# Tying the low parts of causal-attention weights behind the head's scaling on VectorE

## The chip, the cores and the metric

The kernel runs on one core of a Trainium2 chip. The metric is the device time in microseconds, the median of the runs; the kernel before took 1104.67 us (three runs, 1104.64 to 1106.62).

## What is computed

Two layers over 512 tokens of width 1024, in fp32. Layer A mixes tokens by spatial gating, layer B by causal "forgetting" attention with 12 heads of 64; both add attention to a memory of 256 rows (4 heads), a projection back, and a gated feed-forward part of width 2816. The change lies in layer B, of which this is the core:

```python
s_in = rmsnorm(h, ln_shared)
kvf = s_in @ w_shared_kv                 # keys, values, forget gates
k_s = kvf[..., :MAIN_WIDTH].reshape(B, S, FOX_HEADS, HEAD_DIM)
v_s = kvf[..., MAIN_WIDTH:2 * MAIN_WIDTH].reshape(B, S, FOX_HEADS, HEAD_DIM)
log_f_s = jax.nn.log_sigmoid(kvf[..., 2 * MAIN_WIDTH:] + b_forget)
...
logits = jnp.einsum('bthd,bshd->bhts', qi, k).astype(jnp.float32) * scale
logits = logits + ci[..., :, None] - cT[..., None, :]     # c: cumulated log_f
logits = jnp.where(mask, logits, -jnp.inf)
p = jax.nn.softmax(logits, axis=-1).astype(v.dtype)
return jnp.einsum('bhts,bshd->bthd', p, v)
```

## The kernel before

Activations lie transposed, features on the partitions, in tiles of 128 x 512. Each fp32 product is made of three fast ones (mm3, L189 to L193): both factors are split into a high part (a cast to fp32r by ScalarE) and a low part (the rest, a subtraction on VectorE), and high x high, high x low and low x high are added up in PSUM. The split is the helper `split` (L238): `A.copy(hi, src)` and then `tensor_sub(lo, src, hi)`, on VectorE unless told otherwise. In the profile the parts of a weight are called whi and wlo, and the freshly loaded weight raw.

Weights come by `prepared` (L147): a DMA from SP's queue into one of four raw buffers of 128 x 1024, then `weight_parts` (L155), which splits it in steps of 512 columns into whi and wlo tiles; there are eight buffers of each. Weights of another layout, those of the output and of the down projection, go through `moving_pair` (L164), which calls `split` itself. A raw buffer is free for the next load when both of its halves have been cast and subtracted.

In layer B the attention runs over heads in `attend` (L539): four heads on the memory, then the 12 causal heads (FoxHead, L498). For each head the steps stand in a written order:

```python
steps = ("T0", "S3", "F0", "T1", "S2", "N3", "F1", "V0", "S1", "N2", "T2", "F2", "S0", "N1", "V1", "N0",
         "F3", "V2", "F4")
```

S3 to S0 are the logits of the four blocks of 128 queries, the longest row first: two products on TensorE (L513, L514), mask and row maximum in one VectorE instruction (L443), the exponential with its sum on ScalarE (L445). N2 and N0 (`norm`, L448) invert the sums of two blocks (L453) and scale their probabilities (L458): N2 those of blocks 3 and 2, of which block 3 is scaled on ScalarE (L456, by_scalar), N0 those of blocks 1 and 0, both on VectorE. T and V belong to the head before: T0 to T2 transpose its scaled probabilities on TensorE (L465) and split them into pT, V0 to V2 multiply them with the values (L533); behind V2 the output is joined (L423, L424). F0 to F4 are places for other work. They take the copies of queries and keys for heads to come (`pair_split`, `head_parts`, L1342 to L1360, eight small DMAs a head on SP), and pieces of the fill queue: the products of the key blocks (L1240) and value blocks (L1266), cut in 48 pieces, from which heads take 5, 5, 5, 5 (the memory heads), 4, 4, 4, 4, 3, 3, 3, 3 (the first eight causal ones), and then of the output projection. `queue` (L214) lists the load of a block, with its splits, three pieces ahead of the block's first. The fill queue is value block 0, keys 0 and 1, value block 1, keys 2 and 3, value block 2, keys 4 and 5.

The order in which the program lists instructions isn't the order in which an engine gets them. When the kernel is built, a scheduler simulates the engines and gives each of them, among the listed instructions whose inputs and buffers are there, the earliest listed one. So instructions that are listed late are put ahead of earlier ones that still wait for something. `tc.issue_after(ins)` (in the helper `behind`, L247) is the tool against that: whatever is listed in its block for the same engine as `ins` is put in that engine's queue behind `ins`. It adds no semaphore and concerns no other engine. An engine works its queue off in the order given.

Of the kernel before, what the change touches and what calls it, by code (L numbers as in the profile page):

```python
# [40 lines left out]
def hybrid(ctx: ExitStack, tc: tile.TileContext, i: dict, out: bass.AP):  # L41
# [8 lines left out]
    pp = ctx.enter_context(tc.tile_pool(name="psum", bufs=3, space=PSUM))  # L50

    n_of = {}
    last_load, last_exp, last_parts = [None], [None], [None, None]

    def name(s):
        n_of[s] = n_of.get(s, 0) + 1
# [20 lines left out]
    V, A, PE, G = nc.vector, nc.scalar, nc.tensor, nc.gpsimd  # L77
# [53 lines left out]
    def pair_of_parts(n=512, aside=False):  # L131
        if aside:
            return act("whi"), act("wlo")
        return (wp.tile([P, max(n, 512)], F32R, tag="hi", name=name("whi"), bufs=8)[:, :n],
                wp.tile([P, max(n, 512)], F32R, tag="lo", name=name("wlo"), bufs=8)[:, :n])

    def cut(pair, w):

        return [(pair[0][:, d : d + w], pair[1][:, d : d + w]) for d in range(0, pair[0].shape[1], w)]
# [7 lines left out]
    def prepared(src, shape, aside=False):  # L147

        raw = wp.tile([P, 1024], F32, tag="raw", name=name("raw"), bufs=4)
        n = shape[0] * shape[1]  # L150
        dst = raw[:, :n].rearrange("p (a b) -> p a b", a=src.shape[1]) if len(src.shape) == 3 else raw[:, :n]
        last_load[0] = nc.sync.dma_start(dst, src)
        return weight_parts(raw, shape, aside)

    def weight_parts(raw, shape, aside=False):  # L155
        n = shape[0] * shape[1]
        parts = []
        for d in range(0, n, 512):
            pair = pair_of_parts(min(512, n - d), aside)
            split(raw[:, d : min(d + 512, n)], *pair)  # L160
            parts += cut(pair, shape[1])
        return parts

    def moving_pair(src, aside=False):  # L164

        raw = wp.tile([P, 1024], F32, tag="raw", name=name("raw"), bufs=4)
        last_load[0] = nc.sync.dma_start(raw.rearrange("p (m c) -> p m c", m=4), src)
        four = raw.rearrange("p (m k c) -> p m k c", m=4, k=2)
        parts = []
        for x in range(2):  # L170
            hi, lo = (t.rearrange("p (m c) -> p m c", m=4) for t in pair_of_parts(aside=aside))
            split(four[:, :, x, :], hi, lo)
            parts.append((hi, lo))
        return parts
# [60 lines left out]
            for dst, src in src_dst:  # L235
                nc.sync.dma_start(dst, src)

    def split(src, hi, lo, eng=None):  # L238
        last_parts[:] = A.copy(hi, src), (eng or V).tensor_sub(lo, src, hi)  # L239

    def scaled_parts(src, g, hi, lo):

# [3 lines left out]
    @contextmanager  # L246
    def behind(some):  # L247

        with ExitStack() as s:
            for ins in some:  # L250
                s.enter_context(tc.issue_after(ins.ins))
            yield
# [124 lines left out]
    def mem_project(layer, xs, wk):  # L377
        keys = []
        wv = [prepared(i["w_mem_v"][layer, kh], (4, 256)) for kh in range(2)]
        for m in range(2):  # L380
            [o] = group([wk[m]], xs, (0, NMEM), ["mm"])
            kf = temp("memk", (P, NMEM))
            V.tensor_mul(kf, o, rmem)
            for j in range(2):
                own, other = rows(j)
                both = act("memk", shape=(P, 2, NMEM))
                A.copy(both[own, 0, :], kf[own, :])
                V.tensor_sub(both[own, 1, :], kf[own, :], both[own, 0, :])
                if layer:
                    G.dma_start(both[other, :, :].bitcast(F32), both[own, :, :].bitcast(F32))  # L390
                else:
                    A.copy(both[other, 0, :], kf[own, :])
                    V.tensor_sub(both[other, 1, :], kf[own, :], both[own, 0, :])
                keys.append(both)
        vals = []
        for mt in range(2):
            o = ps("mm", (P, 256), s="memv")
            for k in range(KT):
                w = wv[k // 4][k % 4]
                mm3(o, (xs[k][0][:, mt * P : (mt + 1) * P], xs[k][1][:, mt * P : (mt + 1) * P]),  # L400
                    w, k == 0, k == KT - 1)
            vf = temp("memv", (P, 256))
            A.activation(vf, o, AF.Copy, scale=r4m[:, mt : mt + 1])
            vals.append(act("memv", shape=(P, MH, 2, 64)))
            split(vf.rearrange("p (a b) -> p a b", a=MH), vals[mt][:, :, 0, :], vals[mt][:, :, 1, :])
        return keys, vals
# [20 lines left out]

    class Softmax:

        by_scalar = ()  # L430

        def __init__(self):
            self.nmx, self.sm = small("nmx"), small("sm")
# [14 lines left out]
        def norm(self, tb):  # L448

            if tb % 2:  # L450
                return
            with ExitStack() if tb else tc.high_priority():
                V.reciprocal(self.sm[:, tb : tb + 2], self.sm[:, tb : tb + 2])  # L453
                for x in (tb + 1, tb):
                    if x in self.by_scalar:
                        A.activation(self.p[x], self.p[x], AF.Copy, scale=self.sm[:, x : x + 1])  # L456
                    else:
                        V.tensor_scalar_mul(self.p[x], self.p[x], self.sm[:, x : x + 1])  # L458

        def turn(self, n, pieces):  # L460

# [36 lines left out]
    class FoxHead(Softmax):  # L498

        TURNS = ((0,), (1, 3), (2,))  # L500
        by_scalar = (3,)

        def __init__(self, pr, j, vals, dst):
            super().__init__()
# [996 lines left out]
```

## Time and profile before

| | |
|---|---|
| median of three runs | 1104.67 us (1104.64 to 1106.62) |
| profiled execution | 1104.15 us, span 1102.4 us |
| TensorE's granted clock | 0.999 |
| causal heads | about 612 to 720 us of the span |
| scalings of the causal heads on VectorE (L458) | 36, 278 to 421 ns each |
| wlo<-raw on VectorE (L239), whole kernel | 460, median 685 ns |
| 512 KB weight loads on SP in 560 to 725 us | 17 |

PE is TensorE's multiplying and PEld its weight load, which runs beside it; DVE is VectorE, ACT ScalarE, SPq the DMA queue of SyncE. A row of the timeline has start and duration in us, the engine, the line in the kernel, the operation, output<-inputs by the program's names with shapes, and a count where equal ones in a row are merged; in brackets stands how long the engine was idle before it and what ended that. A row of the waits says who waited for what, the total in us, how often, and the longest. The lines themselves stand in the prediction, where they are used.

### The profile page before, as it was taken

The page shows a single profiled execution, that of the slowest core. Times are in us where ns is not written, and L with a number is a line of the kernel's source. Part 1 is how long each engine was busy: PE and PEld are TensorE (multiplying, and loading weights), DVE is VectorE, ACT ScalarE, POOL GpSimd, SP SyncE. Part 2 cuts the span into 40 slices and gives each one's busy share as a digit, 9 for nine tenths or more (in the row PEclk, how much of TensorE's full clock was granted, in tenths as well). Part 3 has the DMA queues.
Part 4 walks back from the last instruction along what each step waited for, and adds up shares of the span by engine and source line. Part 5 has one row for each costly group of instructions (what it writes and reads, how often), then busy time and mean ns, then how long its engine had stood idle before and what let it go on. Part 6 is the DMA issues. An engine that isn't in the chain of part 4 may idle for free.

```text
span 1102.4 us, 19497 instructions
## 1 busy us (share of the span) xinstructions
PE 1094.9 (99%) x7362; PEld 1001.0 (91%) x7363; DVE 887.8 (81%) x1750; ACT 679.7 (62%) x1428; POOL 23.9 (2%) x40
## 2 busy tenths in 40 slices
PE   9999999999999999999999999999999999999998
PEld 8998889999899899998988998889999899899996
DVE  7879759997698488797968789868997698588776
ACT  7776578664365254477747788868665266255454
POOL 0000000000000000001000000000000000000000
PEclk9999999999999999999999999999999999999999
DMA  7521331334135133245222654531235134233232
GB/s 271 160 78 58 115 115 39 116 115 138 54 115 148 53 106 115 77 153 175 73 80 61 154 130 125 148 115 40 78 97 153 58 114 132 62 114 117 77 97 77
DMA packets 64021, 118.65 MB, mean 108 GB/s; under 512 B 5236, under 2 KB 40072, under 8 KB 63928
## 3 DMA queue, kind: packets, MB, share of 16 engines
q1 hardware_dynamic: 63032, 116.57, 34.7%
q8 instruction: 58, 0.95, 0.4%
q0 software_dynamic: 192, 0.52, 0.2%
q10 hardware_dynamic: 704, 0.32, 0.1%
q14 instruction: 35, 0.29, 0.1%
HBM read 105.23 MB, written 2.10 MB: 97 GB/s over the span
## 4 chain that ended last, share of the span: by engine, by line
PE 95%; DVE 2%; ACT 2%; DMA 0%; issue 0%; SPq 0%; DVEq 0%; ACTq 0%
PE y L191 10%; PE y L192 10%; PE y L193 10%; PE a L191 5%; PE a L193 5%; PE a L192 5%; PE ps L191 4%; PE ps L193 4%; PE ps L192 4%; PE e L191 3%; PE e L193 3%; PE e L192 3%; PE x L193 3%; PE x L191 3%; PE x L192 3%; PE v L191 2%
## 5 line engine op out<-in xcount | busy, mean ns | idle before, releaser
L239 ACT CAST whi<-raw 128x512 fp32r<-128x512 f32 x460 | 277.6, 620 | 260.3 <-PE y L193 118.5
L239 DVE TENSOR_TENSOR wlo<-raw,whi 128x512 fp32r<-128x512 f32 x460 | 306.3, 686 | 116.8 <-ACT whi L239 114.7
L191 PE MATMUL y<-whi,fhi 128*128 128x512 f32 (+1 forms) x356 | 139.6, 393 | 0.0
L193 PE MATMUL y<-whi,flo 128*128 128x512 f32 (+1 forms) x356 | 139.4, 391 | 0.0
L192 PE MATMUL y<-wlo,fhi 128*128 128x512 f32 (+1 forms) x356 | 139.2, 391 | 0.0
L193 PE MATMUL x<-xshi,wlo 128*128 128x256 f32 x320 | 89.8, 281 | 0.0
L191 PE MATMUL x<-xshi,whi 128*128 128x256 f32 x320 | 89.7, 280 | 0.0
L191 PE MATMUL a<-xshi,whi 128*128 128x256 f32 x320 | 89.7, 281 | 0.0
L192 PE MATMUL a<-xslo,whi 128*128 128x256 f32 x320 | 89.7, 280 | 0.0
L192 PE MATMUL x<-xslo,whi 128*128 128x256 f32 x320 | 89.7, 280 | 0.0
L193 PE MATMUL a<-xshi,wlo 128*128 128x256 f32 x320 | 89.6, 281 | 0.0
L193 PEld LDWEIGHTS y<-whi,flo 128*128 128x128 f32 x356 | 66.9, 188 | 15.6 <-DVE flo L239 0.2
L192 PEld LDWEIGHTS y<-wlo,fhi 128*128 128x128 f32 x356 | 66.9, 188 | 14.9 <-DVE wlo L239 0.2
L191 PEld LDWEIGHTS y<-whi,fhi 128*128 128x128 f32 x356 | 66.9, 188 | 14.7 <-ACT fhi L239 0.2
L191 PE MATMUL ps<-xshi,whi 128*128 128x256 f32 (+1 forms) x224 | 68.4, 305 | 0.0
L192 PE MATMUL ps<-xslo,whi 128*128 128x256 f32 (+1 forms) x224 | 66.7, 298 | 0.0
L193 PE MATMUL ps<-xshi,wlo 128*128 128x256 f32 (+1 forms) x224 | 66.3, 298 | 0.0
L191 PEld LDWEIGHTS a<-xshi,whi 128*128 128x128 f32 x320 | 60.3, 188 | 0.3
L192 PEld LDWEIGHTS a<-xslo,whi 128*128 128x128 f32 x320 | 60.2, 188 | 0.4
L191 PEld LDWEIGHTS x<-xshi,whi 128*128 128x128 f32 x320 | 60.2, 188 | 0.0
L193 PEld LDWEIGHTS x<-xshi,wlo 128*128 128x128 f32 x320 | 60.2, 188 | 0.0
L193 PEld LDWEIGHTS a<-xshi,wlo 128*128 128x128 f32 x320 | 60.2, 188 | 0.0
(303 smaller groups left out, 3075.1 us busy)
## 6 DMA issues: line engine op xcount, KB each, us to landing
raw<-in_w_gate SPq DMA_DIRECT2D x44, 512.0 KB, 3.6
raw<-in_w_up SPq DMA_DIRECT2D x44, 512.0 KB, 3.6
raw<-in_w_down SPq DMA_DIRECT2D x44, 512.0 KB, 4.0
raw<-in_w_out SPq DMA_DIRECT2D x16, 512.0 KB, 4.0
raw<-in_w_b_q SPq DMA_DIRECT2D x8, 512.0 KB, 4.3
raw<-in_w_a_v SPq DMA_DIRECT2D x6, 512.0 KB, 8.1
raw<-in_w_a_u SPq DMA_DIRECT2D x6, 512.0 KB
raw<-in_w_v SPq DMA_DIRECT2D x6, 512.0 KB, 3.5
```

Of the source, the lines that this page charges most:

```text
L191: PE.matmul(o, w[0], x[0], start=start, stop=False, skip_group_check=more)
L192: PE.matmul(o, w[0], x[1], start=False, stop=False, skip_group_check=more)
L193: return PE.matmul(o, w[1], x[0], start=False, stop=stop, skip_group_check=more)
L239: last_parts[:] = A.copy(hi, src), (eng or V).tensor_sub(lo, src, hi)
```

## The change

`split` gets a flag, pinned, which `weight_parts` sets. With it the VectorE subtraction is listed behind the last scaling of a causal head; the high part on ScalarE is listed as before. The list last_scaling is shared with FoxHead and overwritten with each VectorE scaling that `norm` lists; the memory heads have a list of their own that nobody reads. Until the first causal head lists a scaling, it is empty.

```diff
-    last_load, last_exp, last_parts = [None], [None], [None, None]
+    last_load, last_exp, last_parts, last_scaling = [None], [None], [None, None], []
...
         for d in range(0, n, 512):
             pair = pair_of_parts(min(512, n - d), aside)
-            split(raw[:, d : min(d + 512, n)], *pair)
+            split(raw[:, d : min(d + 512, n)], *pair, pinned=True)
             parts += cut(pair, shape[1])
...
-    def split(src, hi, lo, eng=None):
-        last_parts[:] = A.copy(hi, src), (eng or V).tensor_sub(lo, src, hi)
+    def split(src, hi, lo, eng=None, pinned=False):
+        first = A.copy(hi, src)
+        with behind(last_scaling if pinned else ()):
+            last_parts[:] = first, (eng or V).tensor_sub(lo, src, hi)
...
     class Softmax:
-        by_scalar = ()
+        by_scalar, scaled = (), []
...
-                        V.tensor_scalar_mul(self.p[x], self.p[x], self.sm[:, x : x + 1])
+                        self.scaled[:] = [V.tensor_scalar_mul(self.p[x], self.p[x], self.sm[:, x : x + 1])]
...
     class FoxHead(Softmax):
         TURNS = ((0,), (1, 3), (2,))
-        by_scalar = (3,)
+        by_scalar, scaled = (3,), last_scaling
```

## Prediction

> **What bounds the kernel now.** I read the page first, then the stretch in which the change acts by windows and by the waits, then the order of VectorE's queue there in the timeline.
>
> ```profile
> span 1102.4 us, 19497 instructions
> PE 1094.9 (99%) x7362; PEld 1001.0 (91%) x7363; DVE 887.8 (81%) x1750; ACT 679.7 (62%) x1428; POOL 23.9 (2%) x40
> ```
>
> TensorE (PE) is busy for 1094.9 of 1102.4 us. The profiled execution took 1104.15 us, 1.75 us of it outside the span; the median of the runs is 1104.67 us, 0.52 us above it. I work out differences within the span and add them to the median.
>
> The causal heads run from 612 to 720 us. In a row of the windows view the columns are the stretch, its length, then the busy time of PE, PEld (weight load), DVE (VectorE) and ACT (ScalarE). Below it stand the waits in the same stretch in which VectorE can have a part, the total first, then how often and the longest.
>
> ```profile
> 611.00:712.00 101.00, 100.36 (x623) 87.96 (x622) 88.96 (x254) 86.00 (x213) 0.00 (x0) 1.00 0.53 137
> PEld o L533 <- DVE pT L239: 1.5, 5, 0.6
> PEld tr L465 <- PE k L193: 0.6, 1, 0.6
> PE tr L465 <- DVE p L458: 0.2, 1, 0.2
> PE o L533 <- DVE pT L239: 0.2, 1, 0.2
> ```
>
> VectorE has 88.96 us of work in 101 us, so some 12 us are free there, and TensorE is idle for only 0.64 us. TensorE or its weight load waits for VectorE by name for 1.5 + 0.2 + 0.2 = 1.9 us (the 0.6 us row is the same instant as the 0.2 us wait of tr). So 1.9 us is the most that any better order on VectorE can win in this stage, and 1104.67 - 1.9 = 1102.8 us the end of the range below. A wait of VectorE itself, however long, costs nothing until one of these rows grows.
>
> What a measurement of this kernel can tell from no change is about 0.2%, or 2.2 us: faster means below 1102.5 us and slower above 1106.9 us. The largest gain that the waits allow is already inside "the same".
>
> **Which instructions the change moves.** Only weight_parts gets pinned=True, and the list that it ties to is empty until the first causal head has scaled. From then on it holds the last scaling that VectorE was given. Five loads of the fill queue are listed in that time: key blocks 2 and 3 at piece 21 (head 0) and 25 (head 1), both value weights of block 2 at piece 29 (head 2), key blocks 4 and 5 at piece 37 (head 4) and 41 (head 5). I count the causal heads from 0. With attend's steps the first three come in F2, behind N2, whose VectorE scaling is that of block 2; the last two come in F3 and F4, behind N0. Each load of 1024 columns gives two low parts (wlo), so twelve are tied. The output weights go through moving_pair and aren't; the gate and up weights after the last head are tied to a scaling that has long run.
>
> Which wlo in the trace belongs to which load follows from the order of the loads on SP and the four raw buffers, which go round:
>
> ```profile
> 569.19 6.22 SPq L152 DMA_DIRECT2D raw<-in_w_k  x2
> 588.12 2.63 SPq L152 DMA_DIRECT2D raw<-in_w_v  x2
> 609.96 0.54 SPq L152 DMA_DIRECT2D raw<-in_w_k  x1
> 622.98 0.53 SPq L152 DMA_DIRECT2D raw<-in_w_k  x1
> 625.94 0.39 SPq L167 DMA_DIRECT2D raw<-in_w_out  x1
> ```
>
> These are key blocks 2 and 3, the two value loads, key 4, key 5 and the first output weights. So the next twelve wlo on VectorE are, in that order (x2 is a pair):
>
> ```profile
> 603.09 0.69 DVE L239 TENSOR_TENSOR wlo<-raw,whi 128x512 fp32r<-128x512 f32 x1
> 605.55 0.68 DVE L239 TENSOR_TENSOR wlo<-raw,whi 128x512 fp32r<-128x512 f32 x1
> 620.49 1.29 DVE L239 TENSOR_TENSOR wlo<-raw,whi 128x512 fp32r<-128x512 f32 x2
> 622.31 0.69 DVE L239 TENSOR_TENSOR wlo<-raw,whi 128x512 fp32r<-128x512 f32 x1
> 625.19 0.68 DVE L239 TENSOR_TENSOR wlo<-raw,whi 128x512 fp32r<-128x512 f32 x1
> 628.01 0.69 DVE L239 TENSOR_TENSOR wlo<-raw,whi 128x512 fp32r<-128x512 f32 x1 [0.63 <-ACT whi L239]
> 631.34 0.68 DVE L239 TENSOR_TENSOR wlo<-raw,whi 128x512 fp32r<-128x512 f32 x1
> 638.53 0.68 DVE L239 TENSOR_TENSOR wlo<-raw,whi 128x512 fp32r<-128x512 f32 x1
> 640.37 0.69 DVE L239 TENSOR_TENSOR wlo<-raw,whi 128x512 fp32r<-128x512 f32 x1
> 657.71 1.29 DVE L239 TENSOR_TENSOR wlo<-raw,whi 128x512 fp32r<-128x512 f32 x2
> ```
>
> The output load of 625.94 starts just as the second value wlo ends (625.19 + 0.68), which bears the mapping out. The scalings that they get tied to are those of heads 0, 1, 2, 4 and 5:
>
> ```profile
> 617.08 0.42 DVE L458 TENSOR_SCALAR p<-p,sm 128x384 f32<-128x384 f32 x1
> 626.65 0.41 DVE L458 TENSOR_SCALAR p<-p,sm 128x384 f32<-128x384 f32 x1
> 635.67 0.41 DVE L458 TENSOR_SCALAR p<-p,sm 128x384 f32<-128x384 f32 x1
> 655.84 0.55 DVE L458 TENSOR_SCALAR p<-p,sm 128x256 f32<-128x256 f32 x2
> 663.62 0.86 DVE L458 TENSOR_SCALAR p<-p,sm 128x384 f32<-128x384 f32 x3
> ```
>
> All twelve stand ahead of their scaling now and must move: key 2 by 14 and 12 us, key 3 by 6, the values by 13 to 5, key 4 by 18 and 16, key 5 by 7. No instruction is added or dropped, and the tie is an order in one queue, not a semaphore; VectorE's total stays 887.8 us. A pair takes 1.29 us and one 0.69, so each further one holds the queue for 0.60 us.
>
> **What each move costs.** Listed earlier than the next logits, a tied part whose inputs are there will, I expect, be issued as soon as the scaling is out, ahead of that head's last mask (block 0) and of the sums and scaling behind it; what waits there is the head's first transposes on TensorE.
>
> ```profile
> 618.13 0.29 DVE L443 CUSTOM_DVE_ANT_0 p<-lg,neg 128x128 f32<-128x128 f32 x1 [0.62 <-PE lg L514]
> 619.20 0.55 DVE L458 TENSOR_SCALAR p<-p,sm 128x256 f32<-128x256 f32 x2
> 621.30 0.60 PE L465 MATMUL tr<-ident,p 128*128 128x128 f32 x4
> 636.31 0.29 DVE L443 CUSTOM_DVE_ANT_0 p<-lg,neg 128x128 f32<-128x128 f32 x1 [0.23 <-PE lg L514]
> 637.04 0.69 DVE L239 TENSOR_TENSOR wlo<-k,whi 128x512 fp32r<-128x512 f32 x1 [0.43 <-ACT whi L239]
> 638.07 0.54 DVE L458 TENSOR_SCALAR p<-p,sm 128x256 f32<-128x256 f32 x2
> 639.75 0.60 PE L465 MATMUL tr<-ident,p 128*128 128x128 f32 x4
> 680.85 0.55 DVE L458 TENSOR_SCALAR p<-p,sm 128x256 f32<-128x256 f32 x2
> 681.54 0.63 PE L465 MATMUL tr<-ident,p 128*128 128x128 f32 x4 [0.20 <-DVE p L458]
> ```
>
> The last two rows are a place where the transposes do wait: they start 0.14 us after the scaling ends (680.85 + 0.55).
>
> Head 0: the scaling frees VectorE at about 617.4, two parts take it to 618.6, the mask starts 0.5 us later than 618.13, and the last scaling ends at 620.25 in place of 619.75. TensorE asks at 621.30: covered, cost 0. If that 1.5 us of cover were gone, the 0.5 us would show whole.
>
> Head 1: the same with two parts, the mask 1.1 us later. But the value part of 628.01, which waited 0.63 us for ScalarE with the reciprocal queued behind it, is gone from this place, so most of the shift comes back: cost 0.
>
> Head 2 is the place that matters, for four parts land behind one scaling. VectorE is free at 636.0, four parts take 2.4 us, to 638.4. From mask to scaling took 619.20 - 618.13 = 1.07 us in head 0, where nothing stood between. So the scaling starts at 638.4 + 1.07 = 639.5 and ends at 640.05; with those 0.14 us TensorE transposes at 640.2, 0.45 us later than 639.75. If the low part of the keys (637.04) gets in ahead as well, 0.60 us more: 1.05. If the mask is put between the tied parts, nothing. As bounds: 0, and 2.4 us, all four uncovered. I take 0.45, from the shortest measured chain, since the two parts of key 4 (638.53, 640.37) leave just this place and the backlog is worked off behind it.
>
> Head 4: two parts (1.2 us) come behind 656.3 where key 5's two (657.71) leave: an exchange, cost 0.
>
> Head 5: key 5's pair starts at 664.4 and with the 0.68 us that joins the head's output ends near 666.25, where the mask of the next head now starts:
>
> ```profile
> 666.10 0.69 DVE L443 CUSTOM_DVE_ANT_0 p<-lg,neg 128x512 f32<-128x512 f32 x1 [0.65 <-PE lg L514]
> ```
>
> That is 0.15 us late at the head of the stretch in which the chain that ended last runs over VectorE and ScalarE, so I count it whole. Bounds: 0, and 0.60 for one part that meets no gap.
>
> The sum: 0 + 0 + 0.45 + 0 + 0.15 = +0.6 us, and 1104.67 + 0.6 = 1105.3 us. By itself this case spans 1104.2 to 1106.3 (its two ends 0 and 1.05 + 0.60, and half a microsecond between runs).
>
> The Trainium skill (Trainium Kernel Development and Optimization, Best Practices) says that matmul busy time is a poor measure of the distance to the limit and the weight load's share a good one. By that share, 87.96 of 101 us, up to 13 us would be open here. The waits above, 1.9 us, don't bear it out, and it changes the chance of a gain alone.
>
> **The rivals.**
>
> A. No cost, or a little gain. The schedule puts the mask between the parts, or gives TensorE other work while the transposes wait. For it: VectorE has 12 us free in the stage. A gain needs one of the 1.9 us of waits to shrink; they lie late, among unpinned output weights, which speaks against it. 1104.7 us, at best 1102.8. Chance 0.33.
>
> B. SP is held up, slower. A raw buffer is free only when its second low part has run. The first output load stands on SP ahead of the copies for head 3:
>
> ```profile
> 627.08 0.48 SPq L1357 DMA_DIRECT2D qc<-whi  x1
> 630.89 1.19 SPq L1357 DMA_DIRECT2D ka<-whi  x2
> ka<-whi SPq DMA_DIRECT2D x24, 128.0 KB, 2.4
> ```
>
> If it keeps that place while the value parts go behind head 2's scaling, it waits until 637.2; the eight copies, 5.0 us from first to last, end at 642.3 and land 2.4 us later, at 644.7. Head 3's logits come right behind the transposes of 639.75, at 640.1: 4.6 us lost, 1109.3 us. It decides once the load's wait ends later than about 632.7. Against it: the loads are put in the queue where their buffer comes free. Chance 0.08.
>
> C. All four parts of head 2 uncovered, TensorE without other work: 1104.67 + 2.4 = 1107.1 us. Chance 0.03.
>
> D. A gain over 2.2 us: the order shifts all over the program, or the loader's idle time is worth something after all. If all 101.00 - 87.96 = 13.0 us were, 1091.6 us; but TensorE itself is idle for 0.64 us of them only. Chance 0.05.
>
> E. The tie changes nothing, because the parts were behind already: 1104.7 us. The rows exclude that for all twelve. Chance 0.02.
>
> **How the numbers follow.** The forecast has 0.49. The same: 0.49 + 0.33 + 0.02 = 0.84; slower: 0.08 + 0.03 = 0.11; faster: 0.05. The range goes from the end of A (1102.8) to the price of C (1107.1) and leaves out B and D, 0.13.
>
> **What would show it.** In the profile after: twelve wlo behind the scalings as listed; four in a row behind head 2's, with that head's last mask some 2 us behind its logits, and its transposes idle before on DVE p for about 0.45 us; the two at 603 and 605 gone. TensorE's idle time in 611 to 712 near 1.2 us in place of 0.64. Wrong would be: waits of o on pT that shrink (A with a gain), logits that wait for a copy (B), or a changed order of TensorE outside the heads (D).

## The result and the profile after

The changed kernel takes 1107.74 us (median of 12 runs, 1106.37 to 1109.03), the kernel before beside it 1104.66 us (12 runs, 1103.84 to 1106.62): a ratio of 1.0026, with a 95% interval of 1.0018 to 1.0034. It is slower by 3.1 us, where 0.6 us were forecast and 2.2 us is what a measurement can tell. Some executions of the same kernel have a mean granted clock of 0.997 or 0.998 in place of 0.999 or more and take 1.5 to 2 us longer: two of the changed kernel's 12 here and four of the seven of e1 below, whose median they raise. The profiled execution took 1106.37 us, 2.22 us more than that of before. First the page's totals, then the windows view of the heads' stretch (length, then busy time of PE, PEld, DVE and ACT), then the waits there in which VectorE has a part.

```profile
span 1104.6 us, 19495 instructions
PE 1097.1 (99%) x7363; PEld 1001.9 (91%) x7363; DVE 887.6 (80%) x1750; ACT 679.3 (61%) x1428; POOL 24.3 (2%) x40
```

```profile
611.00:712.00 101.00, 99.75 (x614) 86.67 (x613) 88.09 (x250) 84.62 (x209) 0.00 (x0) 1.00 0.52 137
```

```profile
PEld o L535 <- DVE pT L241: 0.9, 4, 0.4
PE tr L467 <- DVE p L460: 0.7, 2, 0.5
```

TensorE's idle time in the stretch went from 0.64 to 101 - 99.75 = 1.25 us, close to the 1.2 that the prediction named, and the waits on VectorE by name fell from 1.9 to 1.6 us. Yet the same 101 us hold 614 products in place of 623. So neither view shows the whole loss. What does is the distance from start to start. I use three measures, worked out from the starts of TensorE's products in each trace:

- **heads**: from the first 512-column logits of causal head 0 to the last transposition;
- **last stage**: from the first to the last 256-column product of layer 1's feed-forward part;
- **pitch**: mean time from one 256-column product to the next in that stage, the longest 5% left out.

| | before | after | difference |
|---|---|---|---|
| start of head 0 | 612.86 us | 612.51 us | -0.35 |
| heads | 104.30 us | 105.75 us | +1.45 |
| last stage | 286.57 us | 287.61 us | +1.04 |
| pitch there | 117.34 ns | 117.83 ns | +0.49 |

The first row is lost or won in the first 50 us, where executions differ, and both traces then run alike to head 0. The first three rows make 2.14 of the 2.22 us. The medians are 3.1 us apart; what lies between isn't in this pair of profiles.

In the heads, the places are these. Intervals from one head's first logits to the next's, in us:

| | 0 | 1 | 2 | 3 | 4 | 5 | 6 | 7 | 8 | 9 | 10 |
|---|---|---|---|---|---|---|---|---|---|---|---|
| before | 8.79 | 9.24 | 9.22 | 9.34 | 7.91 | 7.99 | 7.85 | 8.73 | 6.18 | 8.41 | 8.91 |
| after | 9.15 | 9.24 | 8.87 | 10.42 | 7.93 | 8.61 | 7.49 | 8.15 | 6.76 | 8.67 | 8.71 |

Heads 0 and 1 of the changed kernel in VectorE's timeline:

```profile
617.08 1.29 DVE L241 TENSOR_TENSOR wlo<-raw,whi 128x512 fp32r<-128x512 f32 x2
618.28 0.29 DVE L445 CUSTOM_DVE_ANT_0 p<-lg,neg 128x128 f32<-128x128 f32 x1
618.49 0.69 DVE L241 TENSOR_TENSOR wlo<-q,whi 128x512 fp32r<-128x512 f32 x1
620.01 0.67 DVE L241 TENSOR_TENSOR wlo<-k,whi 128x512 fp32r<-128x512 f32 x1
620.60 0.54 DVE L460 TENSOR_SCALAR p<-p,sm 128x256 f32<-128x256 f32 x2
626.52 1.29 DVE L241 TENSOR_TENSOR wlo<-raw,whi 128x512 fp32r<-128x512 f32 x2
628.78 0.55 DVE L460 TENSOR_SCALAR p<-p,sm 128x256 f32<-128x256 f32 x2
```

Two rows stand there that the prediction didn't have: the low parts of the next queries and keys, between the mask and the last scaling. In the kernel before they had run long before (and at head 2 the one of the queries):

```profile
611.80 0.69 DVE L239 TENSOR_TENSOR wlo<-q,whi 128x512 fp32r<-128x512 f32 x1
615.90 0.69 DVE L239 TENSOR_TENSOR wlo<-k,whi 128x512 fp32r<-128x512 f32 x1
634.22 0.68 DVE L239 TENSOR_TENSOR wlo<-q,whi 128x512 fp32r<-128x512 f32 x1
```

They aren't tied to anything. But they take their low buffer from the same eight (`pair_of_parts`), and they are listed behind the tied parts, so a buffer comes to them only after those (e4 below tests this, and finds it at head 0). At head 2 of the changed kernel, VectorE and then TensorE:

```profile
636.03 1.29 DVE L241 TENSOR_TENSOR wlo<-raw,whi 128x512 fp32r<-128x512 f32 x2
637.23 0.42 DVE L241 TENSOR_TENSOR pT<-tr,pT 128x256 fp32r<-128x256 f32 x1
637.56 1.28 DVE L241 TENSOR_TENSOR wlo<-raw,whi 128x512 fp32r<-128x512 f32 x2
638.76 0.29 DVE L445 CUSTOM_DVE_ANT_0 p<-lg,neg 128x128 f32<-128x128 f32 x1
638.97 0.69 DVE L241 TENSOR_TENSOR wlo<-q,whi 128x512 fp32r<-128x512 f32 x1
640.49 0.67 DVE L241 TENSOR_TENSOR wlo<-k,whi 128x512 fp32r<-128x512 f32 x1
641.08 0.54 DVE L460 TENSOR_SCALAR p<-p,sm 128x256 f32<-128x256 f32 x2
```

```profile
620.84 0.28 PE L193 MATMUL v<-whi,slo 128*128 128x256 f32 x1
621.28 0.63 PE L467 MATMUL tr<-ident,p 128*128 128x128 f32 x4 [0.17 <-DVE p L460]
641.77 1.06 PE L467 MATMUL tr<-ident,p 128*128 128x128 f32 x8 [0.54 <-DVE p L460]
666.36 0.63 PE L467 MATMUL tr<-ident,p 128*128 128x128 f32 x4
```

The first two products with the values in head 5's interval, before and after:

```profile
660.13 0.62 PE L533 MATMUL o<-pT,vals 128*128 128x512 f32 x2
```

```profile
660.88 0.94 PE L535 MATMUL o<-pT,vals 128*128 128x512 f32 x2
```

The transposes of head 0 wait 0.17 us by name. But the product before them starts at 620.84 and such products follow each other every 0.12 us, so 0.33 us are lost. At 641.77 it is 0.70, at 666.36 0.28, and its row names no wait at all. The products with the values at 660.88 take 0.32 us longer than before. These four places lose 1.63 us. By the intervals, heads 0 to 5 lose 1.73 us together and heads 6 to 10 give 0.30 back. The last stage has no such place: its loss comes in small steps all along, with the order of work on TensorE, VectorE, ScalarE and SP as before. Windows of 286 us from the stage's first product, before and after (busy time of PE with its count of products first):

```profile
783.40:1069.40 286.00, 286.00 (x2060) 269.05 (x2059) 229.33 (x391) 148.81 (x293) 0.00 (x0) 1.00 0.34 106
```

```profile
784.61:1070.61 286.00, 286.00 (x2051) 268.82 (x2050) 229.39 (x391) 148.47 (x293) 0.00 (x0) 1.00 0.35 106
```

TensorE is busy for all of it in both, at the same granted clock of 1.00, and does nine products fewer.

### The profile page after: what moved, and what is told of

Same layout as the page of the kernel before. It is cut to its first block, busy times and chain, and to the rows that moved or that the text cites. A ratio compares the mean times of both kernels' runs of the same rounds, so it can differ in the third digit from the quotient of the medians.

```text
span 1104.6 us, 19495 instructions
## 1 busy us (share of the span) xinstructions
PE 1097.1 (99%) x7363; PEld 1001.9 (91%) x7363; DVE 887.6 (80%) x1750; ACT 679.3 (61%) x1428; POOL 24.3 (2%) x40
## 4 chain that ended last, share of the span: by engine, by line
PE 96%; DVE 1%; ACT 1%; DMA 0%; issue 0%; SPq 0%; DVEq 0%; ACTq 0%
PE y L191 10%; PE y L193 10%; PE y L192 10%; PE a L191 5%; PE a L193 5%; PE a L192 5%; PE ps L191 4%; PE ps L193 4%; PE ps L192 4%; PE e L193 3%; PE x L193 3%; PE x L191 3%; PE e L191 3%; PE e L192 3%; PE x L192 3%; PE v L191 2%
## 5 line engine op out<-in xcount | busy, mean ns | idle before, releaser
L239 ACT CAST whi<-raw 128x512 fp32r<-128x512 f32 x460 | 277.3, 620 | 261.6 <-PE y L193 118.8
L241 DVE TENSOR_TENSOR wlo<-raw,whi 128x512 fp32r<-128x512 f32 x460 | 306.7, 689 | 117.1 <-ACT whi L239 114.9
```

Source lines behind the costliest of these rows:

```text
L239: first = A.copy(hi, src)
L241: last_parts[:] = first, (eng or V).tensor_sub(lo, src, hi)
```

## The experiments

Each was run with the kernel before beside it, whose medians were 1104.63, 1104.51, 1104.62 and 1104.67 us in the four series (e1 to e4, e5 to e8, e9 to e12, e13 to e15). Pitch is that of the last stage.

| run | median, us | ratio (95%) | heads, us | last stage, us | pitch, ns |
|---|---|---|---|---|---|
| before | 1104.66 | | 104.30 | 286.57 | 117.34 |
| after | 1107.74 | 1.0026 (1.0018 to 1.0034) | 105.75 | 287.61 | 117.83 |
| e1, after again | 1108.82 | 1.0029 (1.0018 to 1.0040) | 106.06 | 287.61 | 117.82 |
| e2, values alone | 1105.79 | 1.0010 (1.0001 to 1.0019) | 104.91 | 286.97 | 117.50 |
| e3, key block 2 alone | 1105.73 | 1.0009 (1.0000 to 1.0018) | 105.21 | 286.95 | 117.44 |
| e4, after, own buffers | 1108.50 | 1.0032 (1.0019 to 1.0044) | 106.87 | 287.71 | 117.90 |
| e5, before, own buffers | 1107.95 | 1.0030 (1.0019 to 1.0042) | 106.38 | 287.70 | 117.90 |
| e6, before, pools moved | 1104.37 | 1.0000 (0.9991 to 1.0009) | 104.27 | 286.55 | 117.32 |
| e7, output weights tied | 1105.07 | 1.0005 (0.9996 to 1.0014) | 104.72 | 286.77 | 117.33 |
| e8, after, pools moved | 1107.32 | 1.0025 (1.0015 to 1.0035) | 105.85 | 287.61 | 117.82 |
| e9, after, one exchange | 1106.99 | 1.0023 (1.0014 to 1.0032) | 106.26 | 286.96 | 117.45 |
| e10, before, same exchange | 1105.41 | 1.0009 (1.0000 to 1.0018) | 104.31 | 287.30 | 117.80 |
| e11, before, other exchange | 1104.62 | 1.0001 (0.9992 to 1.0010) | 104.29 | 286.58 | 117.35 |
| e12, key blocks 3 to 5 alone | 1106.40 | 1.0018 (1.0009 to 1.0027) | 105.24 | 287.61 | 117.82 |
| e13, before, five exchanges | 1104.15 | 0.9998 (0.9989 to 1.0007) | 104.32 | 286.78 | 117.51 |
| e14, before, gap of 64 bytes | 1104.90 | 1.0005 (0.9997 to 1.0014) | 104.25 | 287.91 | 118.15 |
| e15, before, gap of 128 bytes | 1104.13 | 0.9999 (0.9990 to 1.0008) | 104.26 | 286.69 | 117.49 |

### The heads: what the ties move

**e1**: the changed kernel once more, nothing edited.

> The changed kernel once more. In its first profile the causal heads took 1.44 us longer than before (0.36 at head 0, 0.73 around head 2, 0.35 in the rest), and from 780 us on, where the order of the instructions is that of before, TensorE fell behind by another 1.1 us in small, even steps. Theory 1 (the steps come from where buffers of the change lie, so they belong to the program): again +1.4 in the heads and again about +1.1 behind them; +3 us in the runs. Theory 2 (they are scatter between executions): again +1.4 in the heads, but anything from -1 to +1 behind them; the runs +1.5 to +3.

The last stage came out the same to 0.01 us and the heads to 0.31; the 0.31 is at the transposes behind head 2's last scaling, which lost 1.04 us here and 0.70 there. This execution's first head began 2.7 us later than in the first profile of the same kernel: between 9 and 13 us of the span the granted clock is 0.57 here and 1.00 there, and by 41 us the 2.7 us are complete. So spans of single executions say little, and stretches much. Both losses belong to the program.

**e2**: only value block 2 is tied. **e3**: only key block 2. A flag is handed down from `prepared`:

```diff
-            split(raw[:, d : min(d + 512, n)], *pair, pinned=True)
+            split(raw[:, d : min(d + 512, n)], *pair, pinned=pinned)
...
+                        w.extend(prepared(i["w_v"][j, kh], (4, 256), pinned=j == 2))    # e2
...
+                w.extend(prepared(i["w_k"][m], (KT, P), pinned=m in (2,)))              # e3
```

> Only the four low parts of value block 2 are tied, behind head 2's scaling. If the four parts in front of that head's last mask are the main price, the transposes of head 2 wait as in the changed kernel: +0.7 us around head 2, nothing at head 0, and +0.7 us in the runs, with next to nothing behind the heads. If what counts is the number of tied parts, a third of the price: +0.5 in the heads, spread out, and 1 us in the runs.

> Only the two low parts of key block 2 are tied, behind head 0's scaling. My prediction had this place covered (cost 0). Theory (handing out of buffers): the low parts of the next queries and keys are listed behind the tied ones and get their buffers after them, so they too come between head 0's mask and its last scaling: 0.35 us at head 0, nothing at head 2. Rival (the tied pair alone delays the mask): the mask is 0.5 us late, the transposes are not, 0. TensorE's order is that of before, but the weights behind the heads lie in other buffers: if placement is what slows TensorE there, up to +1 us more.

With the values alone, the heads lose 0.61 us, all around head 2 (its interval 8.87 in place of 9.22, the next 10.29 in place of 9.34), near the 0.7 of the first reading. That reading had next to nothing behind the heads, and the last stage took 0.40 us more. With key block 2 alone, head 0 takes 9.16 us in place of 8.79, as in the changed kernel: its transposes lose 0.34. The prediction had it at nothing, on the ground that 1.5 us of other work covered it; e3's own expectation, 0.35, came true. There is a second loss, of 0.55 us, at head 3, where nothing is tied in this run and nothing was expected: the product with the values waits for pT, in whose way stand low parts that all came later than before.

```profile
643.40 0.40 PE L535 MATMUL o<-pT,vals 128*128 128x512 f32 x1
644.07 0.50 PE L535 MATMUL o<-pT,vals 128*128 128x512 f32 x1 [0.27 <-DVE pT L241]
```

**e4**: the changed kernel with the parts of queries and keys in the buffers of another pool, so that they share none with the tied ones. **e5**: the same in the kernel before, as its control.

```diff
-            pair["q"], pair["k"] = pair_of_parts(), pair_of_parts()
+            pair["q"], pair["k"] = pair_of_parts(aside=True), pair_of_parts(aside=True)
```

> The changed kernel with the high and low parts of queries and keys in buffers of the activations' pool, so that they need not queue for the buffers of the weights. If the handing out of buffers makes most of the price in the heads, head 0 loses nothing, and head 2 0 to 0.4 us: the heads take 0.7 to 1.0 us less than in the changed kernel. If the tied parts themselves are the price, the heads take as long as in the changed kernel.

> The kernel before with one thing changed: the high and low parts of the next head's queries and keys are kept in the other pool's buffers, as in the run with own buffers, and nothing is tied. It is the control for that run (1108.5 us, heads 106.87 us). Theory A, that the tied low parts cost the heads time by holding back the parts of queries and keys that share their buffers: then the losses of the run with own buffers at heads 5, 7 and 9 (intervals of 9.57, 10.32 and 10.6 us) come from the other pool's buffers and not from the ties, and they stand here too: heads near 106.2 to 106.9 us, about 1.5 us or more over the kernel before's 104.30, and the run with own buffers is no more than 0.4 us slower than this one. Rival B, that the ties cost the time whatever buffers the queries and keys have: heads near 104.3 to 104.9 us here, time near 1104.7 us, and the losses of the run with own buffers are those of the ties.

The places came out, the sum didn't. With own buffers head 0 takes 8.79 us again and heads 2 and 3 take 9.40 and 9.34. But heads 5, 7 and 9 grew to 9.57, 10.32 and 10.60, and the control shows the same (10.07, 10.63, 9.86) without any tie. These losses are those of the edit. In head 7 of e5 the low parts of the next queries and keys run among the head's own masks, and the first scaling comes 6.57 us after the head's first logits, where it came after 5.11 in the kernel before. A pair of the output weights stands in front of the last scaling in both (in the kernel before at 678.98). In e5, VectorE and then TensorE:

```profile
678.20 0.69 DVE L239 TENSOR_TENSOR wlo<-q,whi 128x512 fp32r<-128x512 f32 x1
679.28 0.69 DVE L239 TENSOR_TENSOR wlo<-k,whi 128x512 fp32r<-128x512 f32 x1
681.16 1.29 DVE L239 TENSOR_TENSOR wlo<-raw,whi 128x512 fp32r<-128x512 f32 x2
683.20 0.53 DVE L458 TENSOR_SCALAR p<-p,sm 128x256 f32<-128x256 f32 x2
```

```profile
683.88 0.30 PE L465 MATMUL tr<-ident,p 128*128 128x128 f32 x1 [1.32 <-DVE p L458]
```

Against its control the tie costs 106.87 - 106.38 = 0.49 us of heads, where it costs 1.45 with shared buffers. So about 1 us of the 1.45 hangs on the shared low buffers, as far as two such different schedules can be set against each other. That is an argument and not a direct measurement; what e4 shows directly is that the losses of 0.36 us at head 0 and of 0.73 at heads 2 and 3 shrink to 0 and 0.18. The 0.55 us between the times is more than the 0.4 that was allowed (0.43 when each is set against the kernel before beside it).

**e12**: the tie on key blocks 3, 4 and 5 alone (`pinned=m in (3, 4, 5)`).

> The tie is laid on key blocks 3, 4 and 5 alone: those of key block 2 and value block 2 are left out, behind which the low parts of the next queries and keys came late at heads 0 and 2. Theory A, the cost in the heads is that of low parts which come late in front of a scaling: heads 0, 2 and 3 take what they take in the kernel before (8.79, 9.22 and 9.34 us), head 5's interval is the changed kernel's 8.6 in place of 7.99, and in all the heads take 104.6 to 104.9 us. The pairs of buffers in the last feed-forward stage are exactly those of the changed kernel, so by the theory of pairs the stage takes 287.61 us and 117.83 ns all the same, and the time is near 1106.1. Rival B, heads 2 and 3 lose their time even so (the whole is a matter of DVE's order and not of these two blocks): heads 105.4 or more. Rival C for the stage, it follows the heads: 286.9 or less.

Heads 0, 2 and 3 take 8.79, 9.22 and 9.33 us: without the two blocks, the losses of heads 0 and 2 are gone. But the heads took 105.24 us, 0.34 more than the upper end forecast, and the net loss against before is in head 5's interval, 8.93 in place of 7.99 us, where 8.6 was forecast. It is key block 4, which the prediction had called an exchange at no cost: key block 3's head loses nothing (9.24), and key block 5's pair runs only at 666.31, after the loss. Behind head 4's scaling key block 4's pair and then the low parts of queries and keys run, and pT comes behind them all (VectorE, then TensorE):

```profile
656.56 1.29 DVE L241 TENSOR_TENSOR wlo<-raw,whi 128x512 fp32r<-128x512 f32 x2
658.59 0.69 DVE L241 TENSOR_TENSOR wlo<-q,whi 128x512 fp32r<-128x512 f32 x1
659.20 0.68 DVE L241 TENSOR_TENSOR wlo<-k,whi 128x512 fp32r<-128x512 f32 x1
660.41 0.69 DVE L241 TENSOR_TENSOR pT<-tr,pT 128x512 fp32r<-128x512 f32 x1
```

```profile
660.15 0.40 PE L535 MATMUL o<-pT,vals 128*128 128x512 f32 x1
661.15 0.50 PE L535 MATMUL o<-pT,vals 128*128 128x512 f32 x1 [0.60 <-DVE pT L241]
```

**e7**: the same tie on other low parts, those of `moving_pair` (output and down weights), none on `weight_parts`; their unpinned rows stood in front of the one place before where transposes did wait for a scaling.

> The same tie laid on other low parts: those of the output projection's weights (and of the weights behind it) that are made between the last heads, none of those of the key and value blocks. In the profile before, the tr of head 8 and of the heads behind it wait 0.37 us at 680.94, 0.19 at 688.57, 0.26 at 696.51, and o 0.24 at 702.76, with one or two low parts of 0.6 us just ahead of the scaling at 680.85 and 696.30. Theory A, that low parts ahead of a scaling cost TensorE time only where the transposes wait for it, and gain it only if nothing that shares their buffers is late in return: heads 0 to 6 as in the kernel before, up to 0.4 us less at 680 and up to 0.9 us less in all, if the output products that follow don't wait for the low parts; time between 1103.8 and 1104.8. Rival B, that the low parts' own readers are as near as the scaling (the next k and y matmuls): each gain is given back one product later, heads 104.3 to 105, time 1104.7 to 1105.5.

The rival took it. The transposes in front of head 8 no longer wait (interval 7 falls from 8.73 to 8.34 us). Behind them TensorE's order is another, the intervals 8 to 10 are 4.55, 11.12 and 7.99 us in place of 6.18, 8.41 and 8.91, and the heads end 0.42 us later. Part of the gain goes back at once to the reader of a low part itself:

```profile
687.06 0.50 PE L192 MATMUL y<-wlo,mixedhi 128*128 128x512 f32 x1 [0.32 <-DVE wlo L241]
```

### The last stage: where weights lie

A weight's high and low part lie in two of 8 + 8 buffers of the "weights" pool, which stand 2144 bytes apart; I number each eight 0 to 7 by address. The trace has no buffer numbers; they come from the addresses in the built program, product by product. Which low buffer goes with which high one is left over from the order in which buffers were taken before. The tie takes low buffers in another order than high ones, so the pairs of the last stage are others: 284 of the 560 products with a low part there belong to a pair of buffers that the kernel before doesn't have.

**e6** and **e8**: the kernel before, and the changed one, with two pools opened in the other order, which moves all sixteen buffers by 27,648 bytes and leaves the instructions, their order and the pairs. 27,648 is 27 times 1024, so a rule that goes by the rest of an address within 1024 bytes would not show in this move.

```diff
-    tp = ctx.enter_context(tc.tile_pool(name="temps", bufs=4))
     wp = ctx.enter_context(tc.tile_pool(name="weights", bufs=4))
+    tp = ctx.enter_context(tc.tile_pool(name="temps", bufs=4))
```

> The kernel before with the pool of the weight buffers opened ahead of that of the temporaries in place of behind it: every instruction and its order is the same on every engine, only the addresses of the buffers in the on-chip memory differ. It asks about the 1.04 us that TensorE lost in the last feed-forward stage in the changed kernel, where the order of work was that of before and buffers lay elsewhere. Theory A, addresses set the pitch of the matmuls: the stretch of 286.57 us and the pitch of 117.34 ns there move by some tenths of a microsecond and nanosecond or more (either way), the stage of layer 0 (118.12 ns) too, and the heads stay at 104.3 us give or take 0.15. Rival B, what went before sets it (where the engines stand to each other when the stage begins): 286.57 and 117.34 to within 0.1 us and 0.05 ns, and the time stays at 1104.7.

> The changed kernel with the same two pools opened in the other order: its instructions and their order unchanged, other addresses. Theory A, addresses set the pitch in the last feed-forward stage: 287.61 us and 117.83 ns move by some tenths, to about what the kernel before with moved buffers shows; the heads stay at 105.75 to 106.1. Rival B, what went before sets it: 287.61 and 117.83 stay to within 0.1 and 0.05, and the kernel stays 1.0 us behind the kernel before with moved buffers in this stage.

My theory of addresses, as far as a common move can test it, fell: 286.55 and 287.61 us, as without the move. But the other theory, that the stage goes by what the heads did before it, fell with e7, whose heads run differently and whose pitch is 117.33 ns: its pairs are those of before. Sorted by pairs, the runs fall together: the pairing of before gives 286.57, 286.55 and 286.77 us, that of the changed kernel 287.61 (after, e1, e8, and later e12), that of e4 and e5 287.71 and 287.70. Pitches by high buffer (taken within the parts of one weight, without the few products that read t) come out within 0.3 ns where all eight pairs are the same.

**e9** and **e10** turn this into a forecast. In one load of the last stage's first down weights, the two low parts are made in the order second, first; the high parts, and the readers, as before. That exchanges two low buffers; three products of TensorE and some work of ScalarE and VectorE near them change places too. **e11** does it in the next load (`dh == 1`), where no instruction changes its place on any engine but the two subtractions.

```diff
+        if crossed:
+            parts = [...pair_of_parts() for _ in range(2)]
+            for x in range(2):
+                A.copy(parts[x][0], four[:, :, x, :])
+            for x in (1, 0):
+                last_parts[:] = last_parts[0], V.tensor_sub(parts[x][1], four[:, :, x, :], parts[x][0])
+            return parts
...
+        w = [down_weights(layer, 0, dh, crossed=layer == 1 and dh == 0) for dh in range(2)]
```

> The changed kernel with one exchange: of the first down projection's weights of the last feed-forward stage, the low parts of the first block are made in the order second, first (the high parts as before). From there on, which low buffer goes with which high buffer is no longer the pairing of the changed kernel but that of the run with key block 2 alone tied. Theory A, the pitch of TensorE in that stage belongs to the pairs of buffers that hold a weight's high and low part: kernels with the pairing of before took 286.57, 286.55 and 286.77 us there, those with the changed kernel's pairing 287.61 three times, the run with key block 2 286.95. So this one takes 286.95 give or take 0.15, at a pitch of 117.44 give or take 0.05, the 128 matmuls from the high buffer with the shortest pitch back at 115 ns from 119, the heads stay at 105.75 to 106.1, and the time falls by about 0.7 us to near 1107.0. Rival B, the stage's time belongs to what the heads did before it (the kernels with longer heads had the longer stage): 287.61 and 117.83 stay.

> The kernel before with the same exchange and nothing tied: the heads are untouched (104.3 us), the two pairs that result are ones that the runs with the other pool's buffers had, where the high buffer that is short in the kernel before (115.1, 114.9 and 115.2 ns for its three kinds of step) took 118.7, 119.4 and 116.1 ns, and the other 119.4, 118.5 and 118.3 in place of 118.4, 118.5 and 117.9. Theory A, the pairs set the pitch: 64 x (3.6 + 4.5 + 1.0) ns and 48 x (0.9 + 0.4) ns more, about 0.65 us: the stage takes 287.2 give or take 0.15, the pitch is 117.6, and the time 1105.2. Rival B, the history of the heads sets it: 286.57 and 117.34, and 1104.6.

> The kernel before with the exchange in the second block of the same weights: all engines keep their instructions and order to the last one; only two low buffers change places, so that two other pairs result, of which no run so far has a number. Theory A, the pairs set the pitch: the pitch of the matmuls of the two high buffers concerned moves by 0.5 ns or more in at least one kind of step, either way, with up to 0.6 us on the stage, and that of the other six stays within 0.4 ns. Rival B: no buffer's pitch moves by more than 0.4 ns, and 286.57 stays to within 0.1.

e9 came to 286.96 us and 117.45 ns (forecast 286.95 and 117.44), with the heads at 106.26 (up to 106.1 was forecast); e10 to 287.30 (forecast 287.2, at a pitch 0.2 ns above the forecast), with heads that nothing had touched. Windows of 286 us from the first product, of e9 and of e10:

```profile
785.75:1071.75 286.00, 286.00 (x2056) 268.85 (x2055) 230.35 (x392) 148.62 (x293) 0.00 (x0) 1.00 0.34 106
```

```profile
785.89:1071.89 286.00, 286.00 (x2054) 269.04 (x2052) 230.44 (x392) 149.00 (x293) 0.00 (x0) 1.00 0.34 106
```

e11 moved single pitches (high buffer 0 from 119.0, 117.5 and 118.4 ns for its three kinds of step to 117.7, 118.6 and 116.8), but its sum cancelled, 286.58 us, and other buffers moved by up to 0.9 ns where 0.4 was allowed. So the pair sets most of the pitch and not all of it. In e10 too a pair that the exchange left alone moved: high buffer 4 with low buffer 7 takes 116.2, 118.2 and 119.7 ns before and 117.7, 116.8 and 119.3 there.

**e13**: the exchange at five loads of the kernel before, three of them ahead of layer 0's feed-forward stage, so that high buffer 6 gets the short pair's low buffer 2 there too. **e14** and **e15**: a small tile between the two blocks of buffers, 64 or 128 bytes a partition; instructions (but for one memset on GpSimd), order and pairs unchanged. The small tensors behind the low buffers move as well; of what these products read, only t lies there.

```diff
+        hi = wp.tile([P, max(n, 512)], F32R, tag="hi", name=name("whi"), bufs=8)
+        if not spaced:
+            spaced.append(wp.tile([P, 16], F32, tag="spaced", name="spaced", bufs=1))    # e15: 32
+            G.memset(spaced[0][:, :1], 0.0)
```

> The kernel before, nothing tied, with the two low parts of one block made in the order second, first at five places: three ahead of the feed-forward stage of layer 0 and two at the start of that of layer 1. So the pairs of high and low buffers become others in both stages; the order of TensorE's work is that of before but for three products. Theory A, the pair sets the pitch: in the stage of layer 0 the high buffer that takes 119.0, 119.4 and 116.0 ns there (its low partner as in the runs with the other pool's buffers) gets the partner that gave 115.1, 114.9 and 115.2 ns in layer 1, another gets 119.0, 118.5 to 117.x from a pair known from the run with values alone, two are unknown: by the known pairs and 118.3 ns for the unknown, 17 ns less over the eight buffers' three kinds of step, at some 60 matmuls each, so 1.0 us less in layer 0 and 0.2 us more in layer 1: the pitch in layer 0 falls from 118.12 to 117.5 give or take 0.2, and the time to 1103.8 give or take 0.5. Rival B, the shortness of that pair belongs to layer 1's stage and not to the pair: layer 0 stays at 118.1 and the time at 1104.6 to 1104.9.

> The kernel before with 64 bytes a partition left free between the block of the eight high buffers and that of the eight low ones: every instruction, its order and the pairing are those of before; the low buffers lie 64 bytes further from the high ones. It asks what of a pair sets the pitch. Theory A, the distance between the two buffers: the pitches of single buffers move by 1 ns or more, the short pair's 115 ns too, and the stage of 286.57 us by some tenths. Rival B, something else that goes with the pair (which weights stand in it, where the products lie): every buffer's pitch as in the kernel before to within 0.4 ns, 286.57 to within 0.1 us.

> The same with 128 bytes between the two blocks. Theory A, the distance sets the pitch: pitches of single buffers move by 1 ns or more against the kernel before or against the run with 64 bytes (where a distance recurs, so does its pitch). Rival B: as in the kernel before to within 0.4 ns.

The pitch of high buffer 6, in ns, for its three kinds of step (high to high, high to low, low to the next high):

| low buffer | distance, bytes | stage of layer 0 | stage of layer 1 |
|---|---|---|---|
| 2 | 8,576 | 115.0, 115.7, 116.1 (e13) | 115.1, 114.9, 115.2 (before) |
| 3 | 10,720 | | 118.9, 119.3, 118.5 (after) |
| 4 | 12,864 | 119.0, 119.4, 116.0 (before) | 119.3, 119.1, 116.4 (e10) |
| 2, gap of 64 | 8,640 | | 117.8, 117.5, 118.0 (e14) |
| 4, gap of 64 | 12,928 | 114.7, 115.1, 115.4 (e14) | |
| 2, gap of 128 | 8,704 | | 116.1, 116.1, 115.6 (e15) |
| 4, gap of 128 | 12,992 | 118.5, 120.4, 117.8 (e15) | |

In these rows high buffer 6 keeps the pitch of a pair from one stage to the other, to 0.9 ns, and loses it with 64 bytes. With 128 bytes it moves again. Neither buffer sets it alone: the column shows high buffer 6 with three partners, and low buffer 2 gives 117.2, 117.7 and 117.9 ns with high buffer 4 in the changed kernel. e14's last stage takes 287.91 us, 1.34 more than before and more than the change itself cost there, by a gap alone:

```profile
783.15:1069.15 286.00, 286.00 (x2048) 269.06 (x2047) 229.39 (x391) 148.71 (x293) 0.00 (x0) 1.00 0.34 106
```

Its time hardly moves: 1104.90 us, with an interval that holds 1. In part that is because the gap lets layer 0's stage run faster (118.12 to 117.70 ns, and 288.07 to 287.57 us from its first 256-column product to its last). The rest, some 0.6 us, isn't told apart from the scatter of the medians. e13 meets its forecast of the pitch in layer 0 at the edge (117.70 ns; 117.5 give or take 0.2 expected) and that of the time with a median of 1104.15 us, but layer 0's stage is shorter by only 0.34 us (287.73), where 1.0 was forecast. Its interval holds 1: it can't be called faster than before. No version here beats the kernel before by what can be measured.

Which pairs are short stays open. Distance alone isn't it: in the changed kernel two pairs at the same distance of eleven steps (high buffers 1 and 2) take 118.2, 118.5, 117.6 and 117.5, 116.3, 118.8 ns, and at the 10,720 bytes of the second row high buffer 7 with low buffer 4 takes 120.7, 124.9 and 118.8 ns in layer 0 of e13.

## Why the prediction was wrong

**What moves.** The twelve parts moved as listed, each to its scaling; the two at 603 and 605 are gone from there. The step that failed is the list itself: "only weight_parts gets pinned=True" counts the tied instructions and not those that stand behind them for a buffer. The low parts of queries and keys follow the tied ones, at heads 0, 2 and 4.

**Head 0**, forecast 0: this head starts 0.35 us earlier in the profile after. Counted from the head's start, the mask came 0.5 us late (618.28 - 612.51 = 5.77 us, against 618.13 - 612.86 = 5.27), as forecast. But the last scaling ended at 621.14, where 620.25 - 0.35 = 619.90 was forecast, since two low parts of 0.6 us each ran in between. So the scaling is 1.74 us later than in the kernel before, more than the 1.5 us of cover: 0.36 us in the interval. e3 has it alone, and e4 has it gone.

**Head 1**, forecast 0: 9.24 us before and after. Right.

**Head 2**, forecast 0.45, or 1.05 with the key's low part ahead: the mask 2.45 us late (about 2 was said), both low parts ahead, the transposes lose 0.70 us and 1.04 in e1; the intervals of heads 2 and 3 make +0.73. The mechanism was right, its term too small, and the four parts came as two pairs with a pT between.

**Heads 4 and 5**, forecast 0 and 0.15: together +0.62 in head 5's interval. The "exchange" was wrong: key block 4's pair went behind head 4's scaling, but pulled queries and keys behind it, and pT waited. e12 shows it with key block 2 and the values untied.

**The sum** of the heads: 1.45 us in place of 0.6. By TensorE's idle time it would have been exactly the forecast, 0.64 to 1.25. That was luck in part, since 0.17 of the new idle time stands at head 0, where none was forecast; and that view is blind to products that stretch. The same blindness is in the bound of 1.9 us on any gain, which counts idle time and named waits alone. The prediction's own span for this case, 1104.2 to 1106.3, puts the half microsecond between runs on the lower end only; on the upper one it would give 1106.8, still short of 1107.74. The weight load's busy time fell from 87.96 to 86.67 us, by 1.29, while matmul busy time fell by 0.61, so it shows more of the 1.45. The Trainium skill (Trainium Kernel Development and Optimization, Best Practices) tells the reader to judge the distance to the limit by the weight load's busy share and not by matmul busy time. For this comparison the trace agrees; that 13 us were open by it no run bears out.

**Outside the heads**, forecast nothing: 1.04 us. No step of the prediction looked at where buffers lie; it put what lies behind the heads at nothing because the order there stays. e9 (0.65 us back by one exchange), e10 (0.73 us lost by one) and e14 (1.34 us lost by a gap alone) show it to be the placing of high and low buffers.

**The rivals.** A, no cost: no. B, SP held up: no logits waited for a copy. C, 2.4 us at head 2: no. D's mark, another order outside the heads, didn't appear, though another time did, and in the other direction. The case that came, a third kind, was not among them; the range (to 1107.1) missed it by 0.6 us, and slower than 0.2% had a chance of 0.11.

**Left open**: why the stall at head 2 differs between executions of the same order (0.70, 1.04, 1.16 us in after, e1 and e9), the rest of up to 0.9 us between the medians and the two profiles, and what in a pair of buffers makes a product shorter or longer.

## What to carry to other kernels

Where a change holds an instruction back, list what takes a buffer behind it from the same pool: it moves as well, tied or not. Where TensorE is the bound, compare the count of products in equal windows, since idle time and waits by name show only part of a loss. And a change of order also deals out the buffers anew, which here is worth up to 1.1 us in a stage (e4 and e5 against the kernel before), as a gap of 64 bytes is worth 1.3: before a difference of 0.1% is put down to an order, change the placing of the buffers alone.

## What the hardware showed unexpectedly

The pitch of the same 128x128 by 256-column product, with TensorE never idle and the granted clock at 1.00, lies between 114.4 ns (high buffer 6 in e9) and 121.0 ns (high buffer 1 in e4, low to next high) in the last stage, and reaches 124.9 ns in layer 0 of e13 (high buffer 7, high to low). It goes with the pair of buffers that hold the weight's parts, though not with it alone. It comes back to 0.3 ns in other orders with the same eight pairs and after a common move of 27,648 bytes. For high buffer 6 it comes back to 0.9 ns in the other stage, and a shift of 64 bytes between high and low buffers changes it by up to 4.3 ns, one pair up and the other down. The Trainium skill (SBUF — State Buffer, SBUF: two separate sides) says that TensorE's reads of that memory never wait on anyone. These runs don't show whether anything waits there, but the time of a product here isn't a matter of its columns alone.
